# The down projections of two feed-forward networks: ten feature blocks plain, twelve by Strassen

## The chip, the cores and the metric

One core of a Trainium2 chip. The metric is the device time of one launch in microseconds (us). The engines are TensorE (PE, matmuls, with its weight loads as PEld), VectorE (DVE), ScalarE (ACT), GpSimd (POOL), and SyncE (SP), whose queue issues most DMAs. Each engine works through its own instructions in a fixed order and waits at an instruction until its semaphores are there. TensorE's granted clock is given as a share of 2.4 GHz.

## The reference

A decoder layer on 16 meta tokens and 512 tokens (T = 528), float32, model width 1024:

```
h = concat([meta, x])
h = h + 0.5 * swiglu(rmsnorm(h), ffn1_w_gate, ffn1_w_up, ffn1_w_down)   # FFN1
u = rmsnorm(h) @ w_in                                                    # mixer: two kinds of attention
h = h + concat([o_a, o_b]) @ w_out
h = h + 0.5 * swiglu(rmsnorm(h), ffn2_w_gate, ffn2_w_up, ffn2_w_down)   # FFN2
return h[:, 16:]
swiglu(x) = (silu(x @ w_gate) * (x @ w_up)) @ w_down                     # hidden width 2816
```

The hidden width is 22 feature blocks of 128, the model width 8 blocks of 128.

## The kernel before

Every float32 operand is split into a rounded high part and a low rest, and each product is three matmuls: high x high, high x low, low x high. A weight block is loaded by SyncE into one of three raw buffers (class `Weights`, L83), ScalarE copies out its high part (L100), VectorE subtracts to get the low part (L101); there are two high and two low buffers. Activations lie split the same way.

The program is FFN1, mixer, output projection, FFN2. In gate/up of a network (function `ffn`) the first 6 of 22 feature blocks go through plain matmuls (L432, tiles `g` and `u`), the other 16 in pairs through class `Strassen`: for each pair of blocks seven products in the order 1 2 6 5 7 3 4, into three accumulators X, V, Y; VectorE makes the weight sums (L162), ScalarE and VectorE split them (L174, L175), TensorE multiplies 264 (FFN1) or 256 (FFN2) columns at a time (L193). The results are combined in `evac`, made into silu(gate) x up, and split into high and low.

The down projection then is plain. For each of 8 output blocks: load the residual row (`before_down`), run 22 feature blocks x 3 matmuls into `d` (L432; in FFN1 two column halves of 264, in FFN2 one of 512), add half of it to the residual in VectorE (L582), and `post_extra`: in FFN1 the mixer's high part on ScalarE (L324), low part (L325), square and sum of squares (L334, L335), and a save to DRAM (L592); in FFN2 the store to the output (L1277). A weight row of a block is three conversions of 1024, 1024 and 768 elements. Order on every engine comes from a scheduler that places the instructions once, when the program is built.

Of the kernel before, what the change touches and what calls it, by code (L numbers as in the profile page):

```python
# [18 lines left out]
P = 128  # L19
# [26 lines left out]
USL = 16  # L46
# [80 lines left out]
class Strassen:  # L127
# [10 lines left out]
    def load(self):  # L138
        k = self.nload
        self.nload += 1  # L140
        if k >= 2 * len(self.mats):
            if k % RAWS < 3:
                self.after()
            return
        t = self.raw(k)
        self.nc.sync.dma_start(t, self.mats[k // 2][k % 2])
        self.at[k] = t

    def conv(self):
# [10 lines left out]
        def add(o, a, b, op):  # L160
            s[o] = self.sums()
            op(s[o], s[a], s[b])  # L162
# [38 lines left out]
def layer(ctx: ExitStack, tc: tile.TileContext, xT, gcols, kvg, lamv, rel, onehot,  # L201
# [31 lines left out]
    xpl = [AR[:, 7 * NX + i * KC * T: 7 * NX + (i + 1) * KC * T].rearrange("p (c t) -> p c t", c=KC) for i in range(2)]  # L233
    late = [AR[:, i * SW: (i + 1) * SW] for i in range(NF - USL)]
    FA = pool.tile([P, 6624], F32, name="FA")
    R = pool.tile([P, T], F32, name="R")
    sqr = pool.tile([P, 2, T], F32R, name="sqr")
# [4 lines left out]
    sqs, vv = FA[:, 0:T], FA[:, T: 2 * T]  # L242
    TT = [FA[:, 1344 + i * T: 1344 + (i + 1) * T] for i in range(2)]
    tmp = [FA[:, 2400 + i * T: 2400 + (i + 1) * T] for i in range(6)]
    TB = [FA[:, 5568 + i * T: 5568 + (i + 1) * T] for i in range(2)]

    blocks = []
    for wg, wu, wd in ((w1g, w1u, w1d),):
        for f in range(NPL):
            blocks += [wg[f], wu[f]]  # L250
        n_plain = len(blocks)
        for m in range(KC):
            blocks += [wd[m][:, 0:1024], wd[m][:, 1024:2048], wd[m][:, 2048:2816]]
    n_ffn1 = len(blocks)
# [7 lines left out]
    for wg, wu, wd in ((w2g, w2u, w2d),):  # L262
        for f in range(NPL):
            blocks += [wg[f], wu[f]]
        n_plain2 = len(blocks)
        for m in range(KC):
            blocks += [wd[m][:, 0:1024], wd[m][:, 1024:2048], wd[m][:, 2048:2816]]
# [60 lines left out]
    def square_h(m, c0, add):  # L328
        h = res[0]
        if m == 0:  # L330
            A.activation(sqs[:, c0:], h[:, m, c0:], AF.Square)
        else:
            t = TT[m % 2]
            A.activation(t[:, c0:], h[:, m, c0:], AF.Square)  # L334
            add.tensor_add(sqs[:, c0:], sqs[:, c0:], t[:, c0:])  # L335

    def rms_total(goff, c0):

        A.activation(sqr[:, 0, c0:], sqs[:, c0:], AF.Copy)
        V.tensor_sub(sqr[:, 1, c0:], sqs[:, c0:], f32(sqr[:, 0, c0:]))  # L340
# [70 lines left out]
    def ffn(goff, wg, wu, c0, xpl, xq, us, after_first, before_down, post_extra):  # L411
# [5 lines left out]
        us = us + late  # L417
# [18 lines left out]
        xs = [x[:, : 8 * hn].rearrange("p (s k t) -> p s k t", s=2, k=4) for x in xq]  # L436
# [36 lines left out]
        def sums():  # L473
            ring["s"] += 1
            x = ring["s"] % 4
            return hflat[:, x * 512: (x + 1) * 512]

        def raw(k):
# [3 lines left out]
            return hflat[:, 2048 + (k - 3) * 1024: 2048 + (k - 2) * 1024]  # L482
# [11 lines left out]
        def evac(i, p, ps):  # L494
# [25 lines left out]

        mats = [(w[a], w[b]) for a, b in pairs for w in (wg, wu)]
        eng = Strassen(nc, mats, raw, parts, sums, bank, lambda q, s, k: xs[q][:, s, k], evac, ws.load)
# [841 lines left out]
```

## Time and profile before

| | us |
|---|---|
| median of 3 runs | 1066.93 (1065.89 to 1067.57) |
| the profiled execution | 1072.45 |
| its span | 1070.70, mean granted clock 0.983 |
| FFN1 gate/up, by Strassen | 91.0 to 253.2 |
| FFN1 down | 253.2 to 382.1 |
| mixer and output projection | 382.1 to 696 |
| FFN2 gate/up | 696 to 944.6 |
| FFN2 down | 944.6 to 1066.9 |

Stage borders are those at which the chain of waits passes from one tile to another. A row of a profile names an engine, a line of the kernel, the tile written and the tiles read; "x12" counts instructions.

### The profile page before, as it was taken

The numbers are of one execution on the slowest core, as the hardware profiler recorded it, in microseconds if no ns is written. First come the engines' busy times: TensorE is split into PE (matmuls) and PEld (weight loads), VectorE is DVE, ScalarE is ACT, GpSimd is POOL, SyncE is SP. The second block draws the span as 40 slices with busy tenths as digits, with TensorE's granted clock in tenths as the row PEclk, the third lists the DMA queues.
The fourth block names the chain that finished last, engine by engine and source line by source line (L and its number), as shares of the span: only waits on it lengthen the run. The fifth ranks groups of instructions, "written<-read, shape, count | busy, mean of one in ns | idle before, by whom it ended". The sixth has DMA issues, their size and how long they took to land.

```text
span 1070.7 us, 18274 instructions
## 1 busy us (share of the span) xinstructions
PE 1041.6 (97%) x7185; PEld 958.4 (90%) x7185; DVE 764.4 (71%) x1499; ACT 522.4 (49%) x1057; POOL 27.2 (3%) x43
## 2 busy tenths in 40 slices
PE   7989999999999999998999899999999999999998
PEld 7989999999999998998887678788889999988886
DVE  7957999985332346798999978677979999852231
ACT  6624666554222244563546566354546666631121
POOL 0000000000000000000000211000000000000000
PEclk9998999999999999998999789999999999999999
DMA  6263232334333332220220004453343333343331
GB/s 239 81 213 99 99 118 82 117 102 129 117 108 96 116 108 83 75 70 21 89 71 28 21 28 145 158 177 108 100 137 109 108 101 119 125 134 102 122 113 35
DMA packets 38403, 112.58 MB, mean 105 GB/s; under 512 B 4866, under 2 KB 6146, under 8 KB 38316
## 3 DMA queue, kind: packets, MB, share of 16 engines
q1 hardware_dynamic: 36236, 105.64, 30.6%
q0 software_dynamic: 1792, 5.48, 1.5%
q8 instruction: 56, 0.92, 0.4%
q10 hardware_dynamic: 288, 0.29, 0.1%
q14 instruction: 31, 0.25, 0.1%
HBM read 102.98 MB, written 11.44 MB: 107 GB/s over the span
## 4 chain that ended last, share of the span: by engine, by line
PE 87%; DVE 8%; ACT 2%; issue 1%; DMA 1%; ACTq 0%; DVEq 0%
PE d L432 23%; PE X L193 16%; PE V L193 8%; PE u L432 6%; PE g L432 5%; PE nat L708 4%; PE Y L193 4%; PE p_ch L925 3%; PE wo L1162 3%; PE p_ch L664 2%; PE p_ch L1054 2%; PE iq L664 2%; PE p_ch L1162 2%; PE p_s L980 1%; PE p_s L986 1%
## 5 line engine op out<-in xcount | busy, mean ns | idle before, releaser
L101 DVE TENSOR_TENSOR wl<-wr,wh 128x1024 fp32r<-128x1024 f32 (+4 forms) x106 | 120.9, 1142 | 155.7 <-ACT wh L100 154.6
L100 ACT ACTIVATE wh<-wr 128x1024 fp32r<-128x1024 f32 (+4 forms) x106 | 105.4, 995 | 250.2 <-PE d L432 149.2
L432 PE MATMUL d<-AR,wh 128*128 128x264 f32 (+1 forms) x928 | 184.8, 311 | 0.0
L432 PEld LDWEIGHTS d<-AR,wh 128*128 128x128 f32 x928 | 139.6, 188 | 9.7
L193 PE MATMUL X<-AR,ws 128*128 128x256 f32 (+1 forms) x912 | 117.6, 280 | 0.2
L432 PE MATMUL d<-AR,wl 128*128 128x264 f32 (+1 forms) x464 | 115.7, 311 | 0.0
L193 PEld LDWEIGHTS X<-AR,ws 128*128 128x128 f32 x912 | 111.1, 188 | 1.0 <-ACT FA L498 0.8
L174 ACT ACTIVATE ws<-h 128x512 fp32r<-128x512 f32 x140 | 87.7, 628 | 45.9 <-PE X L193 20.3
L175 DVE TENSOR_TENSOR ws<-h,ws 128x512 fp32r<-128x512 f32 x140 | 95.9, 687 | 13.4 <-ACT ws L174 12.2
L432 PEld LDWEIGHTS d<-AR,wl 128*128 128x128 f32 x464 | 75.6, 188 | 4.8
L708 PE MATMUL nat<-wh,hg 128*128 128x256 f32 (+1 forms) x304 | 57.7, 285 | 0.0
L708 PEld LDWEIGHTS nat<-wh,hg 128*128 128x128 f32 x304 | 47.8, 189 | 0.1
L925 PE MATMUL p_ch<-wh,hg 128*128 128x256 f32 x224 | 44.0, 294 | 0.3 <-DVE AR L878 0.3
L708 PE MATMUL nat<-wl,hg 128*128 128x256 f32 (+1 forms) x152 | 43.2, 284 | 0.0
L193 PE MATMUL V<-hg,ws 128*128 128x264 f32 x312 | 42.4, 285 | 0.0
L193 PE MATMUL X<-hg,ws 128*128 128x264 f32 x312 | 42.4, 285 | 0.0
L582 DVE SCALAR_TENSOR_TENSOR h<-d,h 128x528 f32<-128x528 f32 (+1 forms) x16 | 11.2, 700 | 41.1 <-PE d L432 41.1
L432 PE MATMUL d<-hg,wh 128*128 128x512 f32 x128 | 40.0, 393 | 0.0
L193 PEld LDWEIGHTS V<-hg,ws 128*128 128x128 f32 x312 | 39.9, 188 | 0.0
L193 PEld LDWEIGHTS X<-hg,ws 128*128 128x128 f32 x312 | 39.8, 188 | 0.0
L432 PE MATMUL g<-AR,wh 128*128 128x264 f32 x192 | 33.4, 295 | 6.6 <-ACT AR L324 6.6
L193 PE MATMUL V<-AR,ws 128*128 128x256 f32 x312 | 39.6, 277 | 0.0
(310 smaller groups left out, 2266.7 us busy)
## 6 DMA issues: line engine op xcount, KB each, us to landing
wr<-w1u SPq DMA_DIRECT2D x17, 512.0 KB, 3.5
wr<-w2u SPq DMA_DIRECT2D x17, 512.0 KB, 3.4
wr<-w1d SPq DMA_DIRECT2D x16, 512.0 KB, 3.4
wr<-w2d SPq DMA_DIRECT2D x16, 512.0 KB, 3.5
wr<-w2g SPq DMA_DIRECT2D x15, 512.0 KB, 3.5
wr<-w1g SPq DMA_DIRECT2D x14, 512.0 KB, 3.6
wr<-win_n SPq DMA_DIRECT2D x12, 512.0 KB, 3.4
wr<-win_t SPq DMA_DIRECT2D x9, 512.0 KB, 3.5
```

The costliest lines, as they stand in the source:

```text
L100: self.nc.scalar.activation(hi[:, c], r[:, c], AF.Copy)
L101: (low or self.low).tensor_sub(lo[:, c], r[:, c], f32(hi[:, c]))
L174: self.nc.scalar.activation(hi, x, AF.Copy)
L175: V.tensor_sub(lo, x, f32(hi))
L193: self.nc.tensor.matmul(ps, l[:, w], self.rhs(q, r, k), start=(p in FIRST and k == 0 and x == 0), stop=(k == KC // 2 - 1 and x == 2), skip ...
L432: PE.matmul(ps[:, i, : b - a], w[:, k, :], x(kk)[:, a:b], start=(kk == 0 and p_ == 0), stop=(kk == ktot - 1 and p_ == 2))
L582: V.scalar_tensor_tensor(hm, pv(pd), 0.5, hm, op0=OP.mult, op1=OP.add)
L664: PE.matmul(o, w[:, k, :], x[:, k, a:b], start=(k == 0 and p_ == 0), stop=(k == KC - 1 and p_ == 2))
L708: PE.matmul(ps, xx[:, kk, a:b], w[:, k, :], start=(kk == 0 and p_ == 0), stop=(kk == KC - 1 and p_ == 2))
L925: PE.matmul(ps, xx[:, kk, a:b], w[:, kk % 4, :], start=(kk == 0 and p_ == 0), stop=(kk == KC - 1 and p_ == 2))
L1054: PE.matmul(oo, l, r, start=(x == 0), stop=(x == len(seq) - 1))
L1162: PE.matmul(ps, w[:, k, :], x[k0 + k], start=(k == 0 and p_ == 0), stop=(k == nk - 1 and p_ == 2))
```

## The change

In both networks the down projection is split. Feature blocks 0 to 9 stay plain: per output block two steps of five blocks ("pl", 30 matmuls each, two token halves in two banks Z). Blocks 10 to 21 go by Strassen over pairs of output blocks, the two halves of the twelve blocks and the two token halves: seven products of 6 blocks (18 matmuls) for each of four pairs, accumulated in X (products 1, 6, 7, 4), V (5, 3) and Y (2). Steps follow in the order: plain steps with products 1 and 2 ("firsts") of pairs 0 and 1, products 5 6 7 3 4 ("seconds") of pairs 0 and 1, then firsts and seconds of pair 2, of pair 3.

Activations of blocks 10 to 21 stay unsplit until gate/up has ended; seven sums and splits of them (`later`) stand between the first steps. Weights come as rows of 640 (plain) and 768 (products) into six raw buffers, with four weight sums per pair (L639 to L648); conversion (L650, L651) goes two steps ahead into three pairs of buffers. After each product VectorE adds the half result to rows FA (L667). In FFN1 the finished rows of output blocks 0 to 5 are only saved and squared; their split for the mixer (L789 on ScalarE, L792 on VectorE) comes after products 2 and 5 of the last pair, with rows 0 to 3 read back from DRAM. Gate/up itself keeps its products; blocks 10 to 15 are no longer split there, its ring of weight sums is two instead of four, and x is split into `hg` instead of `AR`. One load for the output projection (`war`) is issued during FFN1's down stage instead of at its start.

VectorE in FFN1's down stage before, around one output block (`d` the finished block, `wl` a low weight part, `hg` the mixer's low part, FA the sum of squares):

```order
L582 SCALAR_TENSOR_TENSOR h0_69<-d3_3421,h0_69 128x528
L101 TENSOR_TENSOR wl25_3581<-wr25_3426,wh25_3580 128x1024
L325 SCALAR_TENSOR_TENSOR hg_70<-h0_69,gc_76,hg_70 128x528
L335 TENSOR_TENSOR FA_72<-FA_72 128x528
L101 TENSOR_TENSOR wl26_3635<-wr26_3480,wh26_3634 128x768
L101 TENSOR_TENSOR wl27_3689<-wr27_3534,wh27_3688 128x1024
```

Each block's add, mixer low part and square sum stood between weight conversions.

VectorE in the same stage now, from product 7's conversion in the first run of products 5 6 7 3 4 (L651 conversions, L667 adds, L639/L641/L643 sums for pair 1):

```order
L651 TENSOR_TENSOR wd_3353<-wd_2840,wd_3352 128x768
L667 SCALAR_TENSOR_TENSOR FA_72<-V_3357,FA_72 128x264
L651 TENSOR_TENSOR wd_3379<-wd_2593,wd_3378 128x768
L667 SCALAR_TENSOR_TENSOR FA_72<-X_3013,FA_72 128x264
L639 TENSOR_TENSOR h0_69<-wd_2840,h0_69 128x768
L651 TENSOR_TENSOR AR_71<-h0_69,sqr_77 128x768
L641 TENSOR_TENSOR wd_2840<-wd_2822,wd_2840 128x768
L667 SCALAR_TENSOR_TENSOR FA_72<-X_3013,FA_72 128x264
L643 TENSOR_TENSOR wd_2822<-h0_69,wd_2822 128x768
L651 TENSOR_TENSOR wd_3427<-h0_69,wd_3426 128x768
L667 SCALAR_TENSOR_TENSOR FA_72<-V_3357,FA_72 128x264
L651 TENSOR_TENSOR wd_3454<-wd_2822,wd_3453 128x768
```

The first sum of pair 1 (L639) stands behind the add of product 6 and ahead of product 4's conversion (the row into AR), the next sums between the following conversions and adds.

VectorE at the last pair of FFN1's down stage now, from product 6's conversion (L792 the mixer's low parts, Y the end of product 2, V of product 5):

```order
L651 TENSOR_TENSOR AR_71<-wd_2593,sqr_77 128x768
L792 SCALAR_TENSOR_TENSOR hg_70<-fa2_73,gc_79,hg_70 128x528
L667 SCALAR_TENSOR_TENSOR FA_72<-Y_4101,FA_72 128x264
L792 SCALAR_TENSOR_TENSOR hg_70<-fa2_73,gc_79,hg_70 128x528 x2
L792 SCALAR_TENSOR_TENSOR hg_70<-FA_72,gc_79,hg_70 128x528 x2
L651 TENSOR_TENSOR wd_4131<-wd_2822,wd_4130 128x768
L667 SCALAR_TENSOR_TENSOR FA_72<-V_4134,FA_72 128x264
L792 SCALAR_TENSOR_TENSOR hg_70<-fa2_73,gc_79,hg_70 128x528
L651 TENSOR_TENSOR wd_4159<-h0_69,wd_4158 128x768
L667 SCALAR_TENSOR_TENSOR FA_72<-X_4004,FA_72 128x264
L651 TENSOR_TENSOR AR_71<-h0_69,sqr_77 128x768
```

Five low parts stand ahead of product 7's conversion (L651 `wd_4131`), and that one ahead of the add of product 5 (`V_4134`) and of product 3's conversion (`wd_4159`).

TensorE at the end of FFN1's down stage before, where only `d` follows `d`:

```order
L432 MATMUL d_4053<-AR,wh_4108 128x264 x4
L432 MATMUL d_4053<-AR,wl_4109 128x264 x2
```

and at the same place now, products 6 (the first two rows), 3 and 7:

```order
L695 MATMUL X<-AR,sqr 128x264 x2
L695 MATMUL X<-AR 128x264
L695 MATMUL V<-AR,wd 128x264 x6
L695 MATMUL X<-AR,wd 128x264 x18
L695 MATMUL V<-AR,wd 128x264 x12
```

Six matmuls of product 3 (V) stand ahead of product 7 (the 18 into X), which follows product 6 in the same bank.

The diff, cut to these parts:

```diff
-USL = 16
+NDN = 10
+KS = (NF - NDN) // 2
...
         elif p == 7:
-            add("S3", "A11", "A21", V.tensor_sub)
+            add("S3", "A11", "A21", V.tensor_sub, "A21")
         elif p == 3:
-            add("S4", "A12", "S2", V.tensor_sub)
+            add("S4", "A12", "S2", V.tensor_sub, "S2")
...
-            if f >= USL:
-                o = tmp[f - USL][:, c0 + b * hn: c0 + (b + 1) * hn]
-                V.tensor_mul(o, s, src)
+            if f >= NDN:
+                k = f - NDN
+                V.tensor_mul(sub_(uq[k // KS, b], k % KS, k % KS + 1)[:, 0], s, src)
...
+        def dsplit(q):
+            h, l = dact[q]
+            x = uq[home[q]]
+            for a, b in spans(x, h, l):
+                A.activation(sub_(h, a, b), sub_(x, a, b), AF.Copy)
+                V.tensor_sub(sub_(l, a, b), sub_(x, a, b), f32(sub_(h, a, b)))
+        def dsub(o, a, b):
+            for x, y in spans(uq[o], uq[a], uq[b]):
+                V.tensor_sub(sub_(uq[o], x, y), sub_(uq[a], x, y), sub_(uq[b], x, y))
+        def split_t4():
+            g = wpool.tile([P, 4 * T], F32R, tag="fa1", bufs=1, name="fa1r")
+            dact[T4] = (region((g, KS)), region((AR[:, 8 * UW: 8 * UW + 2 * T], 4), (g[:, UW:], 2)))
+            dsplit(T4)
+        later = {-1: lambda: dsplit(B11), 0: lambda: dsplit(B21), 1: lambda: dsub((0, 0), (0, 1), (0, 0)),
+                 2: lambda: dsub((0, 1), (1, 1), (0, 1)), 3: lambda: dsplit(B22), 4: lambda: dsub((1, 1), (1, 1), (0, 0)),
+                 5: lambda: dsplit(T1), 6: lambda: dsplit(T2), 7: lambda: dsplit(T3),
...
+        PL = NDN * P // 2
+        steps, keys, needs = [], [], {}
+        firsts = [[("pl", i, 0, 0), ("pl", i, 0, 1), (1, i), ("pl", i, 1, 0), ("pl", i, 1, 1), (2, i)] for i in range(KC // 2)]
+        seconds = [[(p, i) for p in (5, 6, 7, 3, 4)] for i in range(KC // 2)]
+        for part in (firsts[0], firsts[1], seconds[0], seconds[1], firsts[2], seconds[2], firsts[3], seconds[3]):
+            steps += part
...
+        def dparts(j):
+            x = (j + 1) % 3
+            if x == 2:
+                return sqr.rearrange("p a t -> p (a t)"), AR[:, X1 - 2 * T: X1]
+            return [wpool.tile([P, WSLOT], F32R, tag=tag, bufs=2, name="wd") for tag in ("whi", "wlo")]
...
+            if p == "pl":
+                x = at_[s][:, :PL]
+            elif p in (1, 2, 4):
+                x = raw_({1: "A11", 2: "A12", 4: "A22"}[p])
+            elif p == 5:
+                V.tensor_add(x, raw_("A21"), raw_("A22"))
+            elif p == 6:
+                V.tensor_sub(raw_("A21"), raw_("A11"), raw_("A21"))
+                x = raw_("A11")
+                V.tensor_sub(x, sums_, x)
+            elif p == 7:
+                x = raw_("A21")
+            elif p == 3:
+                x = raw_("A12")
+                V.tensor_sub(x, x, raw_("A11"))
+            hi, lo = (y[:, : x.shape[1]] for y in dparts(j))
+            A.activation(hi, x, AF.Copy)
+            V.tensor_sub(lo, x, f32(hi))
+            dp[j] = (hi, lo)
+            dfree(*{"pl": [s], 7: [("A21", i)], 3: [("A11", i), ("A12", i)], 4: [("A22", i)]}.get(p, []))
...
+        def dadd(i, a, b, ps):
+            o = row(i, a)[:, b * hn: (b + 1) * hn]
+            V.scalar_tensor_tensor(o, ps, 0.5, o, op0=OP.mult, op1=OP.add)
...
+                for k in range(NDN // 2):
+                    f = c * (NDN // 2) + k
+                    for x, (l, u) in enumerate(((hi, uh), (hi, ul), (lo, uh))):
+                        for b in range(2):
+                            o = c0 + b * hn
+                            PE.matmul(dps["Z"][b], l[:, k * P: (k + 1) * P], u[f][:, o: o + hn],
+                                      start=(f == 0 and x == 0), stop=(f == NDN - 1 and x == 2))
+                if c == 1:
+                    for b in range(2):
+                        dadd(i, a, b, dps["Z"][b])
...
+            h, l = dact[SUMS[p][1]]
+            for k in range(KS):
+                for x, (w, u) in enumerate(((hi, h), (hi, l), (lo, h))):
+                    PE.matmul(ps, w[:, k * P: (k + 1) * P], sub_(u, k, k + 1)[:, 0], start=(p in FIRST and k == 0 and x == 0),
+                              stop=(k == KS - 1 and x == 2), skip_group_check=True)
+            a, b, last = {1: (0, 0, 0), 2: (0, 0, 1), 5: (1, 1, 0), 6: (0, 1, 0), 7: (1, 1, 1), 3: (0, 1, 1), 4: (1, 0, 1)}[p]
+            dadd(i, a, b, ps)
+            if last:
+                done_part(i, a, b, row(i, a))
...
-            for k0, nk in ((0, 8), (8, 8), (16, 6)):
-                if m == 0 and k0 == 8:
-                    for f in range(USL, NF):
-                        u = tmp[f - USL][:, c0:]
-                        A.activation(uh[f][:, c0:], u, AF.Copy)
-                        V.tensor_sub(ul[f][:, c0:], u, f32(uh[f][:, c0:]))
-                mm(pd, *ws.get(), nk, lambda k: uh[k], lambda k: ul[k], k0, NF)
-            hm = halves(res[0][:, m, c0:], n)
-            V.scalar_tensor_tensor(hm, pv(pd), 0.5, hm, op0=OP.mult, op1=OP.add)
-            post_extra(m)
...
+        for j in range(len(steps)):
+            while dn["conv"] <= min(j + 2, len(steps) - 1):
+                dconv()
+            dstep(j)
+            if j in later:
+                later[j]()
+            s = steps[j]
+            if s[0] == 4 and s[1] < 2:
+                residual(s[1] + 2, [row(s[1] + 2, a) for a in range(2)])
...
+        m = 2 * i + a
+        if m < KC - 2:
+            nc.sync.dma_start(hsave[:, m, :], h)
+        else:
+            mix_hi(m, h)
+            mix_lo(m, h)
+            nc.sync.dma_start(hsave[:, m, :], h)
+        if m == 0:
+            sqs[0] = R
+            A.activation(sqs[0], h, AF.Square)
+        else:
+            t = h0flat[:, 3072: 3072 + T]
+            A.activation(t, h, AF.Square)
+            V.tensor_add(sqs[0], sqs[0], t)
...
+        for m in range(KC - 2):
+            if p == "back" and m < KC - 4:
+                nc.sync.dma_start(x[m], hsave[:, m, :])
+            elif p == 2:
+                mix_hi(m, x[m])
+                if m >= 3:
+                    mix_lo(m, x[m])
+            elif p == 5 and m < 3:
+                mix_lo(m, x[m])
```

## Rows read from the trace of the kernel before

**Rows 1.** The page: busy us of each engine, share of the span, instructions.

```profile
PE 1041.6 (97%) x7185; PEld 958.4 (90%) x7185; DVE 764.4 (71%) x1499; ACT 522.4 (49%) x1057; POOL 27.2 (3%) x43
```

**Rows 2.** Windows by stage: length, busy us per engine (instructions), clock, DMA share, GB/s.

```profile
91.00:253.20 162.20, 162.15 (x1324) 161.95 (x1323) 146.64 (x272) 102.44 (x213) 0.00 (x0) 1.00 0.34 110
253.20:382.10 128.90, 128.90 (x1059) 128.90 (x1058) 41.65 (x48) 32.29 (x39) 1.35 (x3) 1.00 0.34 106
944.60:1066.90 122.30, 122.28 (x529) 98.90 (x527) 32.99 (x36) 22.79 (x24) 0.00 (x0) 1.00 0.31 95
```

**Rows 3.** Chain of waits: start us, us, engine, tile and line, instructions.

```profile
97.39 2.96 PE X L193 x24
...
253.21 128.89 PE d L432 x1056
...
809.37 2.72 PE X L193 x24
...
944.61 122.28 PE d L432 x528
```

**Rows 4.** Waits: engine and line, released by: us in total, times, longest.

```profile
ACT wh L100 <- PE d L432: 149.2, 36, 5.0
...
PE u L432 <- DVE wl L101: 3.5, 2, 3.2
```

**Rows 5.** VectorE's lines by shape: count, busy us and mean ns, idle before.

```profile
L101 DVE TENSOR_TENSOR wl<-wr,wh 128x768 fp32r<-128x768 f32 x16 | 15.3, 959 | 58.6 <-ACT wh L100 58.6
...
L335 DVE TENSOR_TENSOR FA<-FA 128x528 f32<-128x528 f32 x14 | 9.9, 704 | 0.4
...
L506 DVE TENSOR_TENSOR FA<-V,FA 128x264 f32<-128x264 f32 x16 | 6.9, 429 | 0.8 <-PE V L193 0.2
...
L506 DVE TENSOR_TENSOR FA<-V,FA 128x256 f32<-128x256 f32 x16 | 6.7, 420 | 0.4 <-PE V L193 0.4
...
L101 DVE TENSOR_TENSOR wl<-wr,wh 128x640 fp32r<-128x640 f32 x8 | 6.5, 816 | 1.4 <-ACT wh L100 1.4
...
L325 DVE SCALAR_TENSOR_TENSOR hg<-h,gc,hg 128x528 fp32r<-128x528 f32 x8 | 6.1, 762 | 0.8 <-ACT hg L324 0.8
...
L450 DVE TENSOR_TENSOR hg<-h,hg 128x1056 fp32r<-128x1056 f32 x4 | 4.9, 1249 | 0.0
```

**Rows 6.** Timelines of VectorE and of SyncE's queue, the end.

```profile
1066.91 0.69 DVE L582 SCALAR_TENSOR_TENSOR h<-d,h 128x512 f32<-128x512 f32 x1 [8.12 <-PE d L432]
...
1067.63 0.34 SPq L1277 DMA_DIRECT2D out_dram<-h  x1
```

**Rows 7.** Timeline of VectorE in FFN2's gate/up, two neighbours.

```profile
908.13 0.68 DVE L162 TENSOR_TENSOR h<-h,wr 128x512 f32<-128x512 f32 x1
908.74 0.68 DVE L162 TENSOR_TENSOR h<-wr 128x512 f32<-128x512 f32 x1
```

**Rows 8.** ScalarE's lines by shape.

```profile
L100 ACT ACTIVATE wh<-wr 128x768 fp32r<-128x768 f32 x16 | 13.5, 846 | 64.6 <-issue 33.1 <-PE d L432 31.5
...
L324 ACT ACTIVATE hg<-h,gc 128x528 fp32r<-128x528 f32 x8 | 5.9, 738 | 4.3 <-DVE h L582 4.3
```

**Rows 9.** DMA issues: KB each, median us to landing.

```profile
wr<-w1d SPq DMA_DIRECT2D x16, 512.0 KB, 3.4
```

**Rows 10.** Timeline of TensorE, a wait in FFN1's gate/up.

```profile
80.01 0.81 PE L432 MATMUL u<-AR,wl 128*128 128x264 f32 x2 [3.20 <-DVE wl L101]
```

**Rows 11.** Windows of 1 us, TensorE: busy (instructions), granted clock, DMA share, GB/s.

```profile
78.00:79.00 1.00, 0.00 (x0) 1.00 0.50 194
79.00:80.00 1.00, 0.00 (x0) 0.55 0.11 42
80.00:81.00 1.00, 0.99 (x4) 0.50 0.08 16
...
85.00:86.00 1.00, 1.00 (x7) 0.53 0.88 328
86.00:87.00 1.00, 1.00 (x10) 1.00 0.29 115
```

More of the change, by code (lines that the diff above doesn't have):

```diff
@@ L141, in load @@
         if k >= 2 * len(self.mats):
-            if k % RAWS < 3:
-                self.after()
+            self.after(k % RAWS)
             return
@@ L158, in conv, with add @@
         s = self.s.setdefault(i, {"A11": r0[:, :512], "A12": r0[:, 512:], "A21": r1[:, :512], "A22": r1[:, 512:]})
-        def add(o, a, b, op):
-            s[o] = self.sums()
+        def add(o, a, b, op, place=None):
+            s[o] = self.sums() if place is None else s[place]
             op(s[o], s[a], s[b])
@@ L261, in layer @@
     blocks += [wob[m] for m in range(KC)]
[L262 to L267, printed above, removed]
+    for f in range(NPL):
+        blocks += [w2g[f], w2u[f]]
+    n_plain2 = len(blocks)
     ws = Weights(nc, wpool, blocks)
@@ L474, in sums @@
             ring["s"] += 1
-            x = ring["s"] % 4
+            x = ring["s"] % 2
             return hflat[:, x * 512: (x + 1) * 512]
@@ L519, in evac, with region, sub_, spans @@
             V.tensor_sub(ul[f][:, o], s, f32(uh[f][:, o]))
+        def region(*places):
+            x, k0 = [], 0
+            for ap, nk in places:
+                x.append((k0, k0 + nk, ap[:, : nk * hn].rearrange("p (k t) -> p k t", k=nk)))
+                k0 += nk
+            return x
+        def sub_(r, a, b):
+            (x, y, ap), = [z for z in r if z[0] <= a and b <= z[1]]
+            return ap[:, a - x: b - x]
+        def spans(*rs):
+            e = sorted({z[1] for r in rs for z in r} | {0})
+            return list(zip(e[:-1], e[1:]))
@@ new lines, in ffn @@
+        KB = KS * P
+        PL = NDN * P // 2
[4 more added lines that the diff above has]
+            steps += part
+        for s in steps:
+            keys += {1: [("A11", s[1])], 2: [("A12", s[1])], 5: [("A21", s[1]), ("A22", s[1])], "pl": [s]}.get(s[0], [])
@@ new lines, in source, with dload @@
+        def source(k):
+            if k[0] == "pl":
+                return wd[2 * k[1] + k[2]][:, k[3] * PL: (k[3] + 1) * PL]
+            a, b = int(k[0][1]) - 1, int(k[0][2]) - 1
+            return wd[2 * k[1] + a][:, NDN * P + b * KB: NDN * P + (b + 1) * KB]
+        free, at_, wraw, gone = [], {}, [], []
+        dn = dict(load=0, conv=0)
+        sums_ = hflat[:, :KB]
+        def dload():
+            while free and dn["load"] < len(keys):
+                k, t = keys[dn["load"]], free.pop(0)
+                dn["load"] += 1
+                nc.sync.dma_start(t[:, : source(k).shape[1]], source(k))
+                at_[k] = t
+            while dn["load"] == len(keys) and wraw and any(wraw[0] is x for x in free):
+                wraw.pop(0)
+                ws.load()
@@ new lines, in dfree, with gate_up_freed @@
+        def dfree(*ks):
+            for k in ks:
+                free.append(at_.pop(k))
+            dload()
+        def gate_up_freed(x):
+            if x < 3:
+                wraw.append(wpool.tile([P, WSLOT], F32, tag="raw", bufs=3, name="wd"))
+                free.append(wraw[-1])
+            elif x == 4:
+                free.extend([hflat[:, 2 * KB: 3 * KB], hflat[:, 3 * KB: 4 * KB]])
+            dload()
+        def dparts(j):
[3 more added lines that the diff above has]
+            return [wpool.tile([P, WSLOT], F32R, tag=tag, bufs=2, name="wd") for tag in ("whi", "wlo")]
@@ L521, in ffn @@
         mats = [(w[a], w[b]) for a, b in pairs for w in (wg, wu)]
-        eng = Strassen(nc, mats, raw, parts, sums, bank, lambda q, s, k: xs[q][:, s, k], evac, ws.load)
+        eng = Strassen(nc, mats, raw, parts, sums, bank, lambda q, s, k: xs[q][:, s, k], evac, gate_up_freed)
         ws.then = eng.load
```

169 lines of the change are left out of this document (115 added, 54 removed).

## The prediction

> **What bounds the kernel now.** I read the page first, then stages, then the chain of waits, then the waits of single engines. The page says that TensorE is busy 97% of the span, VectorE 71%, ScalarE 49% [rows 1], but such shares mix stages, so I cut the span. In the down projection of the first feed-forward network (FFN1, 253.2 to 382.1 us) matmuls fill 128.90 of 128.90 us, VectorE works 41.65 and ScalarE 32.29. In that of FFN2 (944.6 to 1066.9) they fill 122.28 of 122.30, with VectorE at 32.99. In FFN1's gate/up by Strassen, which is the nearest thing the trace has to what the change builds, VectorE works 146.64 of 162.20 us and TensorE still 162.15 [rows 2]. The chain of waits agrees: each down stage is one unbroken piece of matmuls, 1056 of them in 128.89 us and 528 in 122.28 us [rows 3]. ScalarE's and VectorE's weight conversions there wait for TensorE, 149.2 us over the kernel, and the other way round TensorE's waits for a conversion with the largest sum are two, 3.5 us together [rows 4]. So in both down stages the time is the number of matmuls times the time of one, until another engine falls behind.
>
> **What one matmul costs.** 264 columns: 128.89/1056 = 0.1221 us; the Strassen rows of the same width give 2.96/24 = 0.123. 512 columns: 122.28/528 = 0.2316. 256 columns, one weight load each: 2.72/24 = 0.1133 [rows 3]. Half the width costs a little less than half, so twice the weight loads are free at this width. The Trainium skill, "TensorE: Matmul & The Clock Gate", section "Back-to-back issue gap", says otherwise: in streams of weight load and matmul it gives about 81 ns at 128 columns and 131 ns at 512, so narrow matmuls would be poor value; interpolated, an estimate, FFN2's stage would go from 528 x 0.131 = 69 to 984 x 0.098 = 96 us, slower by 27. The rows disagree with it at both widths [rows 3].
>
> **The change, part by part.** Matmuls: a down projection has 22 feature blocks, 8 output blocks, 3 matmuls per product and 2 token halves. Now 10 blocks are plain, 8 x 10 x 3 x 2 = 480, and 12 go through 7 products of 6 blocks for each of 4 pairs, 4 x 7 x 6 x 3 = 504; 984 in each network.
> FFN1: 984 x 0.1221 = 120.1 instead of 128.9, -8.8 us. FFN2: 984 x 0.1133 = 111.5 instead of 122.3, -10.8 us.
> End: the last add is 256 wide (0.42 us) instead of 512 (0.69), and the chain runs matmul, add, store [rows 5, 6], so -0.3 us.
> Together -19.9 us, if nothing waits.
>
> VectorE in FFN1's stage: 16 conversions of 640 (0.816), 28 of 768 (0.959), 16 weight sums of 768 (taken as 0.959 too), 44 adds from PSUM (0.429), splits and differences of the kept activations in 8 pieces of 1056 (1.249), 7 of 528 (0.704) and 6 of 264, the mixer's eight low parts (0.762) and seven square sums (0.704) [rows 5]. That is 13.1 + 26.9 + 15.3 + 18.9 + 17.5 + 6.1 + 4.9 = 102.7 us against 120.1 of matmuls; FFN2, without the last two and a little narrower, 91 against 111.5. Two and a half times as much work as before, but under TensorE's time: on average all of it lies beside matmuls and I cost it at nothing. Were a fifth of it not covered, it would cost 20 us in each network.
>
> The average hides the dense part: the five products 5, 6, 7, 3, 4 of a pair in a row, 90 matmuls, 11.0 us in FFN1 and 10.2 in FFN2. VectorE has 5 conversions and 5 adds beside them, and in the first run of each network also the next pair's 4 sums: 9 x 0.959 + 5 x 0.42 = 10.7 us by durations, 0.5 too many in FFN2. But durations overlap: in a full queue two 512-wide operations of 0.68 start 0.61 apart [rows 7], 0.07 less each, so 14 of them take 10.7 - 1.0 = 9.7 and fit. The Trainium skill, "VectorE: DVE Perf Modes", section "The DRAIN you can't avoid", holds that the next operation does not start until the pipe is empty; by that the 0.5 us would stand in each of such runs. The trace disagrees with it [rows 7]. I take nothing here.
>
> Hand-offs inside a run. Three pairs of buffers hold converted weights, so product 3's conversion starts when product 5 has read its own. In TensorE's new order five or six matmuls of product 3 come ahead of product 7, so TensorE wants it after product 6 and two matmuls: 20 x 0.122 = 2.44 us later (2.27 in FFN2). The conversion takes 0.846 on ScalarE and 0.959 on VectorE [rows 5, 8], 1.81 us and some 0.1 of hops. Covered, unless VectorE is inside another 0.96 us operation: 0 to 0.6 us for each of 7 runs; I take 0.2, +1.4.
>
> The first run of each network has one more wait. Six raw buffers are all held by blocks of pairs 0 and 1, so the last block of pair 1's first sum is asked for only when product 3 of pair 0 is converted, about 2.0 us after product 5's end, and lands 3.4 later [rows 9]. The sum stands in VectorE's queue ahead of product 4's conversion: sum 5.5 to 6.5, conversion until 7.4. TensorE, with 2.2 + 0.6 + 2.2 + 1.6 us of matmuls and two more, wants it at 6.8: 0.6 us. Two further sums stand ahead of product 5 of pair 1 and cost about as much again. 1.2 in each network, +2.4; bounds 0 and a whole landing, 3.4 each.
>
> End of FFN1, the eighth run. After product 2 of the last pair ends (call it 0) ScalarE makes six scaled copies for the mixer, each 0.738 [rows 8], ahead of product 7's conversion, and VectorE's row has five of the low parts ahead of it. ScalarE: 6 x 0.738 + 0.846 = 5.3; VectorE converts until 6.2, then the add of product 5 that product 3's first matmul waits for until 6.7, then one low part until 7.4, then product 3's conversion until 8.4. TensorE does products 5 and 6 until 4.4, waits to 6.7, does two matmuls and waits to 8.4: 2.3 + 1.4 = 3.7 us. With starts 0.07 closer this chain of ten is shorter by 0.7, so 3.0. I take 3.3; bounds 0 (if the copies find gaps) and 3.7. Before, this place has no wait: mixer work for one block at a time sat between conversions.
>
> **The clock.** Before, TensorE stood still from 76.8 to 80.0 us, 3.2 us; its granted clock was 1.00 at 78 to 79, 0.55 in the next slice, 0.50 after that and 0.53 in 85 to 86, full at 86 to 87 [rows 10, 11]. So it went from 2.4 to 1.2 GHz for some 6 us, in which 37 matmuls ended where 10 or 11 per us are usual: 6 - 37/10.5 = 2.5 us lost. The new wait is about as long but broken by two matmuls. Whether the clock falls is open; I put it at two in five and leave it out of the likeliest case.
>
> What I cost at nothing: the later load of one mixer weight, the smaller ring of weight sums in gate/up, the residual rows by pairs (all of it DMA beside stages at 0.34 and 0.31 DMA share [rows 2]); six blocks fewer to split in gate/up, off the chain. The mixer's order on TensorE is unchanged.
>
> **The sum.** On the profiled execution (1072.45 us): 1072.45 - 19.9 + 1.4 + 2.4 + 3.3 = 1059.7. The median of the runs is 1066.93, 5.5 below that execution, and the same terms give 1066.93 - 12.8 = 1054.1; forecast 1054.
>
> **Rivals.**
> 1. All hidden: buffers and scaled copies fall into gaps, 1066.93 - 19.9 = 1047. For it: Strassen gate/up runs at 90% VectorE without a wait [rows 2]. Against: the end of FFN1 is a fixed order. 0.15.
> 2. The clock falls at the end of FFN1, and the wait is the full 3.7: 1054 + 2.5 + 0.4 = 1057. For it: the fall before came in a wait of this length [rows 10, 11]. Against: two matmuls stand in the middle of this one. 0.28.
> 3. Weight loads come late: six raw buffers, four of them held by a pair from its sums to product 4, so at each of the 8 starts of plain steps one landing of 3.4 us shows, less what lies ahead. Half of it, 8 x 1.7 = 13.6 beside the forecast's terms: 1068, no change. For it: the landing is longer than a product. Against: before, the same bytes came in the same stages without a wait in the chain [rows 3], and two plain steps of 30 matmuls each last 7.3 us. 0.10 (half of it within 0.2%, the rest, with fewer landings, below).
> 4. Slower: the look-ahead collapses. VectorE, in order, is a product behind in FFN2's first run of five, so that each conversion stands behind the add of the product before it, and each of the 40 second products pays its own chain, add 0.43 + sum 0.96 + ScalarE 0.85 + conversion 0.96 = 3.2 us, instead of 2.2: 40 x 1.0 = 40 over the clean case, 1087. It decides once VectorE is over one product (2.2 us) behind at the start of a run. For it: 10.7 us of durations against 10.2. Against: the overlap of starts [rows 7], and the plain steps, in which VectorE has 2 x 0.816 + 2 x 0.42 = 2.5 us of work in 7.3. 0.07.
> A quite different failure, unhidden weight loads in FFN2: 984 loads at 98.90/527 = 0.188 each [rows 2] would be 185 us, +73; the gate/up rows with a load per matmul at 0.1133 [rows 3] exclude it.
>
> **How the numbers follow.** The forecast case holds 1050 to 1056 with 0.40. Low end: the clean case less the 1.0 us by which the fastest of the runs lies below their median, 1046. High end: 1047 + 3.7 + 2.5 for the end of FFN1 and + 4.2 + 6.8 for the hand-offs and landings at their worst, 1064. Left out: rival 4, half of rival 3 and a little below, some 0.15. No change within 0.2% (2.1 us, about what a measurement can tell) is 1064.8 to 1069.1: 0.05. Slower 0.07, faster 0.88 (the forecast case, rivals 1 and 2 and half of rival 3).
>
> **What would show it.** Right: both down stages with 984 matmuls each, 0.122 and 0.113 apart; VectorE at 90 to 103 us in each; TensorE waiting for a VectorE conversion in the last pair of FFN1, about 3 us, and a clock slice at 0.5 there if rival 2 holds; FFN2's stage near 113 to 114. Wrong: FFN2's matmuls above 0.12; waits for DMA at the start of plain steps (rival 3); waits at every product (rival 4); a mixer of another length than before.

## The result and the profile after

The changed kernel takes 1055.69 us (median of 4 runs, 1055.50 to 1057.58) where the kernel before takes 1066.88 on the same chip: ratio 0.990, 95% interval 0.9883 to 0.9917, 11.2 us less. The forecast was 1054, 12.9 less.

The chain of waits of the changed kernel, as in [rows 3] (Z are the plain steps, X, V, Y the products, `nat` the first matmuls of the mixer; the first two X rows of pair 0's run are products 6 and 7):

```profile
248.37 7.33 PE Z L682 x60
255.70 2.19 PE X L695 x18
...
288.68 2.21 PE X L695 x18
291.51 2.37 PE X L695 x18
...
371.03 7.31 PE nat L933 x60
...
932.83 7.36 PE Z L682 x60
940.19 2.13 PE X L695 x18
...
992.05 7.09 PE Z L682 x60
```

FFN1's down stage is 371.03 - 248.37 = 122.66 us where it was 128.89. Its matmuls cost what was said: 7.33/60 = 0.1222 and 2.19/18 = 0.1217 us. In FFN2 they do not: 7.09/60 = 0.1182 and 2.13/18 = 0.1183 instead of 0.1133. Windows over the two down stages and the end answer to [rows 2]:

```profile
248.37:371.03 122.66, 121.03 (x986) 120.19 (x986) 92.26 (x135) 49.51 (x67) 1.36 (x3) 1.00 0.42 130
932.83:1050.70 117.87, 117.85 (x984) 116.76 (x983) 82.99 (x123) 39.35 (x51) 0.00 (x0) 1.00 0.37 113
1050.70:1054.10 3.40, 0.00 (x0) 0.00 (x0) 0.42 (x1) 0.00 (x0) 0.00 (x0) 0.93 0.11 39
```

FFN2's stage is 117.87 instead of 122.28. TensorE stands idle 1.63 us in FFN1's stage and 0.02 in FFN2's. Its waits in the down stages are two, both in FFN1:

```profile
PE V L695 <- DVE wd L651: 1.0, 1, 1.0
...
PE V L695 <- DVE FA L667: 0.7, 1, 0.7
```

By stages, profile against profile: FFN1 down -6.2, what lies between the two down stages 562.51 to 561.80 (-0.7; two profiles of one kernel further down, e2_mix_later and e12_mix_later_again, differ by 2.0 there), FFN2 down -4.4, the end (from the last matmul's end to the span's) 3.8 to 3.4 (-0.4): -11.7. FFN1's gate/up ended 4.84 us earlier as well (253.21 to 248.37); the first run below says what that was.

### The profile page after: what moved, and what is told of

Read it like the earlier page. It is cut to its first block, busy times and chain, and to the rows that moved or that the text cites. A ratio compares the mean times of both kernels' runs of the same rounds, so it can differ in the third digit from the quotient of the medians.

```text
span 1054.1 us, 19409 instructions
## 1 busy us (share of the span) xinstructions
PE 1026.3 (97%) x7569; PEld 965.7 (92%) x7569; DVE 862.3 (82%) x1657; ACT 552.5 (52%) x1091; POOL 27.2 (3%) x43
## 4 chain that ended last, share of the span: by engine, by line
PE 87%; DVE 8%; ACT 3%; issue 1%; DMA 1%; ACTq 0%; DVEq 0%
PE X L193 17%; PE Z L682 11%; PE V L193 9%; PE X L695 6%; PE g L435 6%; PE u L435 6%; PE Y L193 4%; PE nat L933 3%; PE V L695 3%; PE wo L1386 3%; PE p_ch L1150 2%; PE p_ch L889 2%; PE iq L889 2%; PE p_ch L1279 2%; PE Y L695 2%; PE p_ch L1386 2%
## 5 line engine op out<-in xcount | busy, mean ns | idle before, releaser
L193 PE MATMUL X<-AR,ws 128*128 128x264 f32 (+1 forms) x1224 | 158.5, 281 | 0.1
L101 ACT ACTIVATE wh<-wr 128x1024 fp32r<-128x1024 f32 (+3 forms) x58 | 57.9, 1000 | 70.7 <-issue 16.1
L102 DVE TENSOR_TENSOR wl<-wr,wh 128x1024 fp32r<-128x1024 f32 (+3 forms) x58 | 66.3, 1146 | 20.6 <-ACT wh L101 20.6
L193 PE MATMUL V<-AR,ws 128*128 128x264 f32 (+1 forms) x624 | 82.0, 280 | 0.0
L193 PEld LDWEIGHTS V<-AR,ws 128*128 128x128 f32 x624 | 77.2, 188 | 0.0
L435 PE MATMUL g<-hg,wh 128*128 128x264 f32 (+1 forms) x288 | 63.9, 330 | 6.6 <-ACT hg L325 6.6
L435 PE MATMUL u<-hg,wh 128*128 128x264 f32 (+1 forms) x288 | 61.4, 322 | 0.0
L435 PEld LDWEIGHTS g<-hg,wh 128*128 128x128 f32 x288 | 46.6, 196 | 11.1 <-ACT hg L325 6.6
L682 PE MATMUL Z<-AR,wd 128*128 128x264 f32 (+1 forms) x432 | 55.1, 284 | 0.0
L682 PEld LDWEIGHTS Z<-AR,wd 128*128 128x128 f32 x432 | 53.2, 188 | 0.4 <-DVE FA L509 0.2
L650 ACT ACTIVATE wd<-h 128x768 fp32r<-128x768 f32 (+1 forms) x28 | 23.0, 823 | 46.8 <-PE Z L682 19.7
L650 ACT ACTIVATE wd<-wd 128x768 fp32r<-128x768 f32 (+1 forms) x30 | 24.2, 808 | 36.2 <-PE Z L682 10.2
```

Of the source, the lines that this page charges most:

```text
L101: self.nc.scalar.activation(hi[:, c], r[:, c], AF.Copy)
L102: (low or self.low).tensor_sub(lo[:, c], r[:, c], f32(hi[:, c]))
L193: self.nc.tensor.matmul(ps, l[:, w], self.rhs(q, r, k), start=(p in FIRST and k == 0 and x == 0), stop=(k == KC // 2 - 1 and x == 2), skip ...
L435: PE.matmul(ps[:, i, : b - a], w[:, k, :], x(kk)[:, a:b], start=(kk == 0 and p_ == 0), stop=(kk == ktot - 1 and p_ == 2))
L650: A.activation(hi, x, AF.Copy)
L682: PE.matmul(dps["Z"][b], l[:, k * P: (k + 1) * P], u[f][:, o: o + hn], start=(f == 0 and x == 0), stop=(f == NDN - 1 and x == 2))
```

## The experiments

Ratios are to the kernel before, run on the same chip in the same set.

**e1_before_again: the kernel before, unchanged**

> The kernel before, unchanged, profiled once more. Theory A: the 3.2 us wait of TensorE at 76.8 us and the half clock after it (some 5 us together) belong to the one profiled execution that was shown, which took 1072.45 us where the median is 1067; another profile shows a landing of the gate weight nearer 7 us than 9.5, a wait of about 1 us, no fall of the clock there, and FFN1's down stage starting near 248.4 instead of 253.2 us. Theory B: the wait belongs to the kernel before, and the change took it away (5 us of its gain): the wait and the start at 253 come again.

1067.43 us in one run, span 1065.6. Its chain of waits, the load before TensorE's wait and FFN1's down stage:

```profile
66.87 7.06 DMA wr<-w1g
...
248.20 128.87 PE d L432 x1056
```

Theory A. The load that took 9.49 us in the profile shown before takes 7.06, as in the changed kernel (7.14), and the down stage starts at 248.20. The wait and the half clock of [rows 10, 11] belonged to that execution, which is why it took 5.5 us more than the median. Spans of this profile and of the changed kernel differ by 1065.6 - 1054.1 = 11.5 us, the medians by 11.2.

**e2_mix_later and e12_mix_later_again: the mixer's copies after products 6 and 7**

```diff
-            elif p == 2:
+            elif p == 6:
                 mix_hi(m, x[m])
...
-            elif p == 5 and m < 3:
+            elif p == 7 and m < 3:
```

> Only the mixer's scaled copies and low parts move: after products 6 and 7 of FFN1's last pair instead of after 2 and 5, so that fewer of them stand ahead of the conversions of products 7 and 3. If the two waits there (0.66 and 0.97 us) come from those rows, they shrink to under 0.5 us together and the kernel is 1.0 to 1.6 us faster, about 1054.5. If they come from something else (the buffers, the look-ahead), they stay, and nothing changes.

Here is first how the two waits arise in the kernel as given: timelines of ScalarE, VectorE and TensorE at the end of FFN1's down stage (start, length, instruction, idle time before and its releaser).

```profile
356.38 2.62 ACT L789 ACTIVATE hg<-fa,gc 128x528 fp32r<-128x528 f32 x4
358.90 1.35 ACT L789 ACTIVATE hg<-FA,gc 128x528 fp32r<-128x528 f32 x2
360.15 0.83 ACT L650 ACTIVATE wd<-wd 128x768 fp32r<-128x768 f32 x1
```

```profile
358.77 1.50 DVE L792 SCALAR_TENSOR_TENSOR hg<-fa,gc,hg 128x528 fp32r<-128x528 f32 x2 [0.38 <-PE V L695]
360.18 1.44 DVE L792 SCALAR_TENSOR_TENSOR hg<-FA,gc,hg 128x528 fp32r<-128x528 f32 x2
361.54 0.95 DVE L651 TENSOR_TENSOR wd<-wd 128x768 fp32r<-128x768 f32 x1
362.41 0.42 DVE L667 SCALAR_TENSOR_TENSOR FA<-V,FA 128x264 f32<-128x264 f32 x1
362.75 0.76 DVE L792 SCALAR_TENSOR_TENSOR hg<-fa,gc,hg 128x528 fp32r<-128x528 f32 x1
363.43 0.95 DVE L651 TENSOR_TENSOR wd<-h,wd 128x768 fp32r<-128x768 f32 x1
```

```profile
362.98 0.48 PE L695 MATMUL V<-AR,wd 128*128 128x264 f32 x2 [0.66 <-DVE FA L667]
364.43 0.75 PE L695 MATMUL V<-AR,wd 128*128 128x264 f32 x4 [0.97 <-DVE wd L651]
```

From VectorE's conversion for product 7 (361.54) on, this is the predicted chain: that conversion, the add of product 5, one low part, product 3's conversion. Its first link is another. I had ScalarE as the limit, with six copies and product 7's conversion after the end of product 2. But the copies (L789) began at 356.4, some 1.5 us before that end, and start 0.63 apart instead of 0.74, so ScalarE has finished both by 361.0. VectorE's low parts (L792) last until 361.6, the second of them held up by 0.38 us until matmuls of product 5 had read their operand in `hg`, where it is written. So 1.63 us instead of 3.3.

With the copies later both waits are gone. FFN1's stage, by the same borders of the chain:

```profile
248.29 7.33 PE Z L682 x60
...
369.31 7.33 PE nat L933 x60
```

121.02 us, 1.64 less, all that was there. The time: 1055.84 us, ratio 0.989 (0.9874 to 0.9907), and in the second set

> The second run once more, on the chip of the run beside it, to price the mixer's copies alone: 1.6 us under the kernel as given by its stage, ratio to the kernel before about 0.989. The difference between this run and the one beside it is what the places in FFN2 are worth, 0 to 2.4 us.

1056.98, ratio 0.9897 (0.9882 to 0.9912), with a stage of 121.05 us. The stage agrees to 0.1 us; the whole shows no more than some of it, within its interval. What hid the rest is not shown, but other places vary by as much: between the two down stages these two profiles take 561.9 and 563.9 us, and in some executions FFN2 has a wait of its own. In the profile of e2_mix_later, the chain and VectorE's timeline in FFN2's first run of products:

```profile
971.26 4.63 DMA wd<-w2d
```

```profile
975.92 0.96 DVE L639 TENSOR_TENSOR h<-wd,h 128x768 f32<-128x768 f32 x1 [2.48 <-DMA wd<-w2d]
```

The first sum of pair 1 waits for its last block, and TensorE then 1.7 us for product 7's add, three rows behind it: the wait that was predicted for each network's first run (I had product 4's conversion, the next row, as what TensorE waits for), in this execution and not in the one shown above (there VectorE waits 0.66 and TensorE not at all).

**e3_align_down and e5_align_all: other places for FFN2's operands**

```diff
-        uh, ul = [x[:, :T] for x in us], [x[:, T:] for x in us]
+        uh, ul = [x[:, :n] for x in us], [x[:, n: 2 * n] for x in us]
...
+        uw, ob = KS * hn, (4224 if n > 512 else 4352)
...
-        own = lambda o: region((hg[:, o: o + UW], KS))
+        own = lambda o: region((hg[:, o: o + uw], KS))
...
-    ffn(G_F2, w2g, w2u, w2d, META, [AR[:, X1 + i * SW: X1 + (i + 1) * SW] for i in range(8)] + [hg[:, 3168:4224], hg[:, 7392:8448]]
+    ffn(G_F2, w2g, w2u, w2d, META, [AR[:, 14848 + i * 1024: 14848 + (i + 1) * 1024] for i in range(8)] + [hg[:, 3328:4352], hg[:, 7424:8448]]
```

and in the second of them also, for FFN2 (with the eight slots in `AR` at 14880 instead of 14848):

```diff
+            if n == 512:
+                g = g[:, 16:]
...
+                if x == 2:
+                    return AR[:, 13328:14096], AR[:, 14096:14864]
+                hi = wpool.tile([P, WSLOT], F32R, tag="whi", bufs=2, name="wd")
+                return hi, wpool.tile([P, WSLOT], F32R, tag="wlo", bufs=2, name="wd")[:, 64:]
```

> FFN2's activations for the down stage get other places: slots of 1024 elements and pieces of 1536, so that all its moving operands start a multiple of 256 elements (1 KB) apart, as those of FFN2's gate/up do. The same work in the same order. Theory A, that the place of the moving operand sets the price of a 256-wide matmul (0.1133 us in gate/up, 0.118 in the down stage): FFN2's down stage falls from 117.9 to about 113 us and the kernel to about 1051. Theory B, that VectorE, ScalarE or the DMAs beside it cost TensorE 4%: the same 117.9, 1055.7. Theory C, that the weights' places or the two accumulators in turn do: the same as B.

1054.75 us, ratio 0.9886 (0.9869 to 0.9903). In its profile a plain step goes from 7.09 to 6.90 to 7.04 us and a product stays at 2.12. The window of FFN2's down stage:

```profile
933.40:1052.30 118.90, 117.02 (x985) 115.71 (x983) 82.57 (x123) 39.33 (x51) 0.00 (x0) 1.00 0.37 112
```

TensorE is busy 0.8 us less than as given, about a sixth of the 4.9 that theory A wanted: here the place of the moving operand alone does not set the price.

> As the third run, and more: in FFN2's down stage now the weights' places too. Every moving operand starts at a multiple of 128 bytes, and the three pairs of buffers for converted weights are laid so that nearly all consecutive weight blocks start a multiple of 512 bytes apart, as in gate/up. Same work, same order. If the places of both operands set the price (in the third run one of three buffer pairs reached 113 to 115 ns, the others 117 to 118), all go to 113 to 115 and FFN2's stage to 112.5 to 114 us where the kernel changed as given has 117.9, so about 1052. If the weights' places do not matter, it stays as in the third run, 116.5 to 117 without a wait for weights, about 1054.7.

1055.31 us, ratio 0.989 (0.9871 to 0.9909). The chain late in FFN2's down stage (product 5 of pair 2, a plain step and product 1 of pair 3):

```profile
1010.51 2.12 PE V L703 x18
...
1021.30 7.02 PE Z L690 x60
1028.33 2.04 PE X L703 x18
```

Some products reach 2.04/18 = 0.1133, the price of gate/up; others and the plain steps stay at 0.117 to 0.118. FFN2's stage is 117.7 us with 1.7 us of TensorE's waits in it (the largest, 1.5, behind a late weight), 116.0 without; as given 117.87 with next to none. So the places of moving operand and weights are worth some 2 us of the 4.8 (984 x 0.0049) that the price costs, and in this profile the waits took them back. The 112.5 to 114 us that I expected of both places together did not come.

**e4_gap_gateup: the reverse, in FFN2's gate/up**

```diff
-        xs = [x[:, : 8 * hn].rearrange("p (s k t) -> p s k t", s=2, k=4) for x in ...]
+        gap = 0 if n > 512 else 16
+        xs = [x[:, : 2 * (4 * hn + gap)].rearrange("p (s w) -> p s w", s=2)[:, :, : 4 * hn]... for x in ...]
```

> The other way round: in FFN2's gate/up the low parts of the activations start 16 elements (64 bytes) further on than before, so that high and low parts are no longer a multiple of 1 KB apart. The same work in the same order. Theory A (place of the moving operand): a 12-matmul product goes from 1.36 to about 1.41 us, and the 1344 Strassen matmuls of that stage take 4 to 7 us longer. Theories B and C (other engines, weights, accumulators): 1.36 us stays.

1063.06 us in one run. Products of FFN2's gate/up in its chain of waits, and the same in the kernel as given:

```profile
796.12 1.43 PE X L193 x12
...
798.98 2.84 PE X L193 x24
```

```profile
794.95 1.36 PE X L193 x12
...
797.67 2.72 PE X L193 x24
```

2.84/24 = 0.1183 instead of 0.1133, from nothing but low parts 64 bytes further on. TensorE is busy 159.9 us with the 1344 products' matmuls instead of 153.2. For gate/up this is theory A, and it gives just the price that FFN2's down stage has. Other engines' work was the same, so B and C do not explain this. For the down stage it shows a cause that is enough, not that it is the only one: there e3_align_down got back a sixth.

**e6_order_5_6_3_7_4: a whole product between 6 and 7**

```diff
-for p in (5, 6, 7, 3, 4)]
+for p in (5, 6, 3, 7, 4)]
```

> Only the order of the products of a pair is changed, 5 6 3 7 4 instead of 5 6 7 3 4: a whole product 3 now stands between products 6 and 7, which share a bank, so the wait of product 7 for the add of product 6 (0.18 to 0.2 us each, 8 times) should go; it comes back between 7 and 4, which share that bank too, and the scheduler covers that with matmuls of the next step where there are any. My theory of hand-offs: the gap at 6 to 7 vanishes, a gap of about 0.4 us stays at the end of each network's last pair only, and the freed buffers of product 3 come earlier, so a wait of the first sum of pair 1 for its weights goes too: 1 us faster, about 1054.6. Rival (the gap is no hand-off but TensorE's own switch of bank): the gaps stay, no change.

Slower than as given: 1062.57 us, ratio 0.9952 (0.9934 to 0.9969). In its chain the gap has gone from product 7 and come to product 4 (18 into X after five plain matmuls):

```profile
304.77 2.19 PE X L695 x18
306.96 0.60 PE Z L682 x5
307.57 2.39 PE X L695 x18
```

0.2 us in either place: a hand-off of the bank. What I had missed is the end of a network, where nothing stands between products 7 and 4. TensorE's waits there:

```profile
PE X L695 <- DVE FA L667: 2.5, 2, 1.9
```

In FFN1 product 4 waits 1.9 us for the add of product 7, which stands in VectorE's row behind a weight of the mixer and a square sum; in FFN2 it waits 0.6. What follows in FFN1 is slower too (product 4 took 2.19 us, the mixer's first 60 matmuls 7.31):

```profile
370.09 3.24 PE X L695 x18
373.33 8.04 PE nat L933 x60
```

The granted clock falls from 2.4 to 1.2 GHz about 1 us behind this wait and is back at 375, which costs 1.8 us. FFN1's stage is 124.9, FFN2's 120.2, and another 1.5 us lies between the stages, half of it this clock.

**e7_twice_low: VectorE's cover drawn down**

```diff
             V.tensor_sub(lo, x, f32(hi))
+            if p != "pl" and n == 512:
+                V.tensor_sub(lo, x, f32(hi))
```

> In FFN2's down stage VectorE makes the low part of every product's weights twice (28 operations of 0.96 us more, the result unchanged): VectorE's work there goes from 83 to about 107 to 110 us of 118. If the cover is what I said, a mean, all of it hides but at the hand-offs, where the margin of 0.4 us at product 3 is overdrawn by about 0.5 us in each of 4 runs: 2 to 3 us slower, about 1058. If VectorE were on the path (rival 4), nearly all of it shows: 20 to 27 us slower. If the margins are wider than I think: no change.

1063.96 us in one run. The window of FFN2's down stage:

```profile
932.90:1058.80 125.90, 120.35 (x984) 118.36 (x983) 106.85 (x152) 39.31 (x51) 0.00 (x0) 0.99 0.36 106
```

24 us more of VectorE (82.99 to 106.85) make the stage 8.0 us longer: a third of it shows. TensorE is idle for 5.5 of them; in the other 2.5 it works longer at the same matmuls (120.35 us for 117.85). Most of that is the clock, which fell to 1.2 GHz between 989 and 992 us, behind the longest wait; the 16 matmuls there take 3.53 us, at 0.1183 each 1.89:

```profile
988.46 0.95 PE L697 MATMUL X<-AR,wd 128*128 128x256 f32 x4 [2.43 <-DVE wd L653]
```

```profile
988.46 3.53 PE X L697 x16
```

```profile
989.00:990.00 1.00, 1.00 (x6) 0.50 0.74 230
```

More than the 2 to 3 I expected and far less than all: VectorE is not the bound, but the margins at the hand-offs are thinner than I worked out, and a wait can cost the clock on top.

**e8_as_given, e9_more_raw, e10_all_three, e11_mix_places**

```diff
+            if n == 512 and j == 10:
+                free.extend([hflat[:, 4 * KB: 5 * KB], fa2[:, :KB], fa2[:, KB: 2 * KB]])
+                dload()
```

> The changed kernel as given, once more, as the measure for the next two on the same chip: 1055.7, with a second level about 2 us higher in some executions if the late weights of FFN2's first run of products (1.7 to 2.0 us of TensorE's time in three of five profiles) come and go.

> FFN2's down stage alone gets three more raw buffers from its twelfth step on, in places whose activations are no longer needed, so that the blocks of pair 1's first sum are asked for earlier. If that wait is one for buffers, as I predicted in the part on the first run (and priced at 1.2 us), the first sum of pair 1 no longer waits for a DMA, and the kernel loses the upper level: median 0.3 to 1.0 lower, all runs near 1055. Rival (the landing itself is late because of other traffic, however early it is asked for): the wait and the spread stay.

> The mixer's copies later (second run), operands of FFN2's down stage in the new places (fifth run), and the three raw buffers (the run beside this), together. Theory, the terms add: -1.6 at the end of FFN1, -1.7 in FFN2's matmuls, up to -1.0 for late weights: 1051.5 to 1053. Rival, they hide one another: not under 1054.5.

On one chip: as given 1056.86 (1055.64 to 1059.77, ratio 0.9905, 0.9885 to 0.9926), three more raw buffers 1058.16 (1057.13 to 1060.21, 0.9911), all three 1057.26 (0.9904). As given, the runs spread over 4 us without two clear levels; the profiled one, the fastest, has no wait of TensorE in FFN2's down stage that the list of waits shows. The terms of all three did not add: the rival, not under 1054.5, held. The buffers did not help. VectorE's part of the chain of e9_more_raw says why (L639 is the first sum of pair 1):

```profile
968.74 0.95 DVE h L639
969.69 0.67 DVE FA L667 x2
970.36 0.86 DVE AR L651
971.22 0.34 DVE FA L667
```

Pair 1's first sum no longer waits for a DMA, so that wait was one for buffers, as I had said. But asked for earlier, the sum was also placed earlier in VectorE's fixed row, ahead of the plain step's adds and a conversion of pair 0, and TensorE waits 0.3 us for a conversion behind them. The longer wait lies one pair further on: VectorE's row with the first sum of pair 2, and product 4 of pair 1, which waits for the add behind it:

```profile
989.95 0.96 DVE L639 TENSOR_TENSOR h<-wd,h 128x768 f32<-128x768 f32 x1 [2.14 <-DMA h<-w2d]
```

```profile
991.39 0.36 PE L695 MATMUL X<-fa1r,wd 128*128 128x256 f32 x1 [0.91 <-DVE FA L667]
```

The first sums of pairs 0, 2 and 3 wait 4.4 us for DMAs together. Neither theory as I put it: the wait changed its place.

> The last run without its three raw buffers: the mixer's copies later (second run) and FFN2's operands in the new places (fifth run). FFN1's stage 121.0 (122.7 as given), FFN2's about 115.5 and whatever it waits for its weights (0 to 2 us). If the terms add, 1.6 + 0.4 to 2.4 us under the kernel as given: 1053.5 to 1055.5, the lowest ratio to the kernel before so far. If FFN2 gives in waits what it gains in matmuls, no more than 1.6 under it.

1055.39 us (1053.73 to 1057.54), ratio 0.9882 (0.9862 to 0.9903), 1.6 us under e12_mix_later_again beside it. The lowest ratio of the study, but its interval overlaps that of the kernel as given, and the kernel as given did not run beside it, so it does not decide whether the terms add. In the profile FFN1's stage is 121.0, FFN2's 118.0 with 2.0 us of waits for late weights, so there FFN2 gave in waits what it gained in matmuls. A version that is surely better was not found; the stage times show where one lies.

## Why the prediction was right, and where it was not

**What bounds the stages, and the counts.** Right. Both stages have 984 matmuls, and TensorE is busy for 121.03 of 122.66 and 117.85 of 117.87 us.

**The price of one matmul.** Right for 264 columns (0.1217 to 0.1222). The step that failed is "FFN2: 984 x 0.1133 = 111.5": I took the price from gate/up [rows 3] and named width alone as its cause. The down stage pays 0.1182, 984 x 0.0049 = 4.8 us more. e4_gap_gateup shows that the place of the operands is enough to make that difference, e5_align_all that it can be undone for some products. Why the plain steps kept 0.117, and what sets the rest of this stage's price, is open.

**VectorE beside TensorE.** 92.3 and 83.0 us busy where I had 102.7 and 91 by durations. The durations in these windows add up to 98.4 and 87.9, so 6.1 and 4.9 us are neighbours that overlap, as [rows 7] said, and the rest is work that I counted and the windows do not hold. In the rows above the conversion at 361.54 lasts 0.95 and the add after it starts 0.87 later. The Trainium skill ("VectorE: DVE Perf Modes", section "The DRAIN you can't avoid") states that the next operation waits for an empty pipe, and also, which the prediction left out, that one which is not held starts earlier. The row does not agree with the first, which would give 0.95, and fits the second. All of VectorE's work hides in the mean; e7_twice_low shows that the spare is smaller than the mean suggests.

**Hand-offs inside a run.** The size held, the mechanism did not. I priced product 3's conversion at 0.2 us in 7 runs; no wait for it shows there. What costs is product 7, which waits for the add of product 6 in its bank: 2.37 instead of 2.19 us, 0.18 in 8 runs, 1.4 as well. e6_order_5_6_3_7_4 moved that gap with the bank.

**The first run of each network.** Taken as 1.2 each. Nothing in FFN1. In FFN2 nothing in the profile shown, 1.5 to 2.0 us of TensorE's time in those of e2, e3, e5 and e11: the mechanism is there, but it depends on the landing of the last block, 4.3 to 4.6 us in these four; with 3.9 in e12_mix_later_again TensorE waits 0.3.

**The end of FFN1.** Mechanism right but for its first link, 1.63 us instead of 3.3. Product 7's conversion waits for VectorE's low parts, done 3.7 us after the end of product 2, and not for ScalarE, which I had busy until 5.3 and which was done after 3.1. Removed entirely by e2_mix_later, which moved copies and low parts together and so does not price them apart.

**The clock (rival 2).** Not in the profile shown: windows of 1 us at the wait keep 1.00.

```profile
363.00:364.00 1.00, 0.46 (x2) 1.00 0.56 139
364.00:365.00 1.00, 0.57 (x4) 1.00 0.91 348
```

In e3_align_down, whose FFN1 is the same, it fell:

```profile
364.00:365.00 1.00, 0.87 (x5) 0.81 0.84 324
365.00:366.00 1.00, 1.00 (x7) 0.50 0.01 4
...
368.00:369.00 1.00, 1.00 (x10) 0.99 0.00 0
```

and in e4_gap_gateup too, where FFN1's stage is 124.21 us both times instead of 122.66: 1.5 us. Of the seven profiles with this FFN1 (the first, e3, e4, e5, e7, e8, e9) that is two; I had said two in five, at 2.5 us. My working of that 2.5 was off: each window of [rows 11] also counts a matmul that it shares with its neighbour. From 80 to 86 us there were 27 matmuls, not 37, and by the chains the 44 that begin with the wait's end took 8.28 us there and 5.64 in e1_before_again: 2.6 us.

**The sum.** Predicted: FFN1 -8.8 + 0.6 + 1.2 + 3.3 = -3.7; FFN2 -10.8 + 0.8 + 1.2 = -8.8; end -0.3. Measured: -6.2, -4.4, -0.4, and -0.7 between the stages, less than two profiles of one kernel differ there. So 12.8 against 11.7 by profile and 11.2 by median is in part luck, two errors that nearly cancel: waits in FFN1 taken 2.5 us too large; and in FFN2 4.4 us too little, matmuls 4.8 too cheap, 0.7 for product 7's gaps and 0.6 in the first two plain steps (7.36 and 7.42 us), against 2.0 of waits that did not come; 0.3 stays unexplained.

**By the prediction's own signs.** The counts and FFN1's price came as said. TensorE waited neither for DMAs at the plain steps nor at every product, so rivals 3 and 4 did not come true. FFN2's matmuls (0.118 for 0.113), its stage (117.9 for 113 to 114) and VectorE in it (83 for 90 and more) were not as said, nor was the wait of about 3 us at the end of FFN1.

## What to carry to other kernels

A duration read in one stage need not hold in another where the operands lie differently: when work moves, compare start to start for the same width in both places. In a fixed order, work that is free on average costs where it stands ahead of a hand-off, and here it could be moved away from there at no cost that the stage shows; asking for data earlier may only move a wait, to the next place that wants data or, since what uses it moves up too, to what then stands behind it. And a profiled execution that is far from the median should be taken again before its waits are explained.

## What was not expected of the hardware

64 bytes between high and low parts of the moving operand took a 256-column matmul from 0.1133 to 0.1183 us, with the same work beside it. The same wait of TensorE (two gaps with two matmuls between them) left the granted clock at 2.4 GHz in five profiles and took it to 1.2 for three to four us in two; single waits of 1.9 us (e6_order_5_6_3_7_4) and 2.4 us (e7_twice_low) took it there as well.
